# A two-layer hybrid decoder on one core: h of the SwiGLU stages turned by DMA instead of TensorE

## The chip, the cores and the metric

The kernel runs on one core of one Trainium2 chip. A core has five engines that run side by side and meet at semaphores: TensorE (PE in the profile; PEld is its weight load), VectorE (DVE), ScalarE (ACT), GpSimd (POOL) and SyncE (SP), which here issues nearly all transfers. Sixteen DMA engines move the data. The metric is the device time of one execution in microseconds (us).

## What is computed

Two layers, each `x += 1/2 SwiGLU_1(norm(x))`, then a mixer (gMLP and an indexer-selected attention side by side), then `x += 1/2 SwiGLU_2(norm(x))`, and a final norm. There are 256 tokens, 1024 channels, and 2816 hidden channels in a SwiGLU; everything is float32. Only the SwiGLUs are touched by the change:

```python
def _swiglu(h, w_gu, w_down):
    gate, up = jnp.split(h @ w_gu, 2, axis=-1)
    return (jax.nn.silu(gate) * up) @ w_down
```

So in the kernel's names h = silu(gate) * up, 256 tokens by 2816 channels, and it is the left operand of the down product.

## The kernel before

**Tiling.** Tokens are cut into two row tiles (t = 0, 1) of 128. A SwiGLU's hidden channels are cut into FC = 11 blocks (j) of 256. `proj(tiles, t, ...)` makes gate and up of one block for one row tile: the output is 128 tokens by 512 columns (256 gate, 256 up) in one PSUM bank `acc`, and the contraction over 1024 channels takes 8 steps. To keep float32 accuracy each operand is split into a coarse part (hi, xhi, hh) and the rest (lo, xlo, hl), and each product is three matmuls (`mm3`, L239): 8 x 3 = 24 matmuls for one row tile, 48 for a block. `down(j, t, ...)` multiplies h of a block by the down weights into two banks `dn` of 512 columns: 2 x 2 x 3 = 12 matmuls for one row tile.

**h.** After `proj`, `h_evac` makes h of that row tile: ScalarE the silu (`sg`, L281), VectorE the product (L283). It lies with tokens on partitions. As the left operand of `down` it must have hidden channels on partitions, so `h_trans` (L286 and following) turns its two 128x128 halves by two TensorE transposes (L289) against `ident` into a PSUM bank `tr`; then ScalarE writes the coarse part `hh` (L293) and VectorE the rest `hl` (L294).

**Order.** The software runs one block behind: after the gate/up products of block j come the first row tile's `h_trans` of block j, `down` of block j-1 for t = 0, the second row tile's `h_trans` and `down` of block j-1 for t = 1. Only the first block differs: its two `h_trans` are put into `hooks`, a list of work that `proj` runs (`run_hooks`) after three quarters of its products, here in block 1. The last two blocks' down products are made in `tail` (in the last SwiGLU, in `final`), where the second row tile of the last block is turned between them.

**Weights.** They come as 512 KB tiles into 4 buffers `raw`, loaded by SP (`issue_dma`, L111). `issue_split` makes `hi` on ScalarE (L135) and `lo` on VectorE (L136) in two halves, in 6 buffers each. `done(n)` gives tile n free, splits the next one and issues the load after that. Only the products of the second row tile call `done`, and the second half of `down` for its two tiles. Per block there are four gate/up tiles and two down tiles.

**Queues.** SP issues in the order of the program text: a load stands behind whatever was written before it. The order on TensorE, ScalarE, VectorE and GpSimd is made by a planner that follows the program text where it can; each of these engines then works through its own list in order. In the first block of layer 0 (`first`) the order is written by hand, and weights and inputs are still arriving.

Of the kernel before, what the change touches and what calls it, by code (L numbers as in the profile page):

```python
# [10 lines left out]
F32 = mybir.dt.float32  # L11
F32R = mybir.dt.float32r
I32 = mybir.dt.int32
AF = mybir.ActivationFunctionType
OP = mybir.AluOpType
AX = mybir.AxisListType
# [3 lines left out]
P = 128  # L20
# [4 lines left out]
FC = DFF // 256  # L25
# [20 lines left out]
def hybrid_kernel(ctx: ExitStack, tc: tile.TileContext, a: dict, out: bass.AP):  # L46
    nc = tc.nc
    V, S, G, PE = nc.vector, nc.scalar, nc.gpsimd, nc.tensor
# [3 lines left out]
    wspl = ctx.enter_context(tc.tile_pool(name="wspl", bufs=SPL_BUFS))  # L52
    keep = ctx.enter_context(tc.tile_pool(name="keep", bufs=1))
    work = ctx.enter_context(tc.tile_pool(name="work", bufs=2))
# [3 lines left out]
    def bank(tag, bufs):  # L58
        return psum.tile([P, 512], F32, name=tag, tag=tag, bufs=bufs)
# [60 lines left out]
    def issue_split(before=None):  # L120
        n = state["split"]
        if n >= len(specs):
            return
        while state["dma"] <= n:
            issue_dma()
        _, k, w = specs[n]
        r = raws.pop(n)
        hi = wspl.tile([P, 1024], F32R, name="hi", tag="hi")
        lo = wspl.tile([P, 1024], F32R, name="lo", tag="lo")
        m = k * w  # L130
        for b in range(2):
            c = slice(b * m // 2, (b + 1) * m // 2)
            if before is not None:
                before(b)
            S.copy(hi[:, c], r[:, c])  # L135
            V.tensor_tensor(lo[:, c], r[:, c], hi[:, c].bitcast(F32), OP.subtract)  # L136
        wts[n] = (hi[:, :m].rearrange("p (k w) -> p k w", k=k),
                  lo[:, :m].rearrange("p (k w) -> p k w", k=k))
        state["split"] = n + 1
        issue_dma()  # L140

    def take(count):
        n = state["use"]
        state["use"] = n + count
        while state["split"] < n + count:
            issue_split()
        return list(range(n, n + count))
# [23 lines left out]
    def rsqrt(dst, v, scale, eng, plus=None):  # L171
# [5 lines left out]
        else:  # L177
            eng.tensor_scalar(h, v, plus, 0.5 * scale, op0=OP.add, op1=OP.mult)
        sh = small.tile([P, 1], I32, name="rs_s", tag="rs_s")
        V.tensor_scalar(sh, h.bitcast(I32), 1, None, op0=OP.logical_shift_right)  # L180
        y = small.tile([P, 1], F32, name="rs_y", tag="rs_y")
        eng.tensor_scalar(y.bitcast(I32), sh, -1.0, RSQRT_GUESS, op0=OP.mult, op1=OP.add)
        u = small.tile([P, 1], F32, name="rs_u", tag="rs_u")
# [12 lines left out]
    def stats(t, eng=None):  # L196
        junk = work.tile([P, D], mybir.dt.bfloat16, name="junk", tag="junk", bufs=1)
        ss = small.tile([P, 1], F32, name="ss", tag="ss")
        S.activation(junk, X[t], AF.Square, accum_out=ss)  # L199
        rstd[t] = small.tile([P, 1], F32, name="rstd", tag="rstd", bufs=4)  # L200
# [16 lines left out]
    def split_gain(t, k, v, g, parts=(0, 1)):  # L217
        if 0 in parts:
            S.activation(xhi[t][:, k, :], v, AF.Copy, scale=g)  # L219
        if 1 in parts:  # L220
# [16 lines left out]
    def mm3(dst, shi, slo, whi, wlo, start, stop, between=None):  # L237
        for n, (a1, b1) in enumerate(((shi, whi), (shi, wlo), (slo, whi))):
            PE.matmul(dst, a1, b1, start=start and n == 0, stop=stop and n == 2)  # L239
            if between is not None:  # L240
                between()

    hooks, steps = [], []
# [15 lines left out]
    def proj(tiles, t, w, last, mid=True):  # L259

        ps = bank("acc", 2)
        for q, n in enumerate(tiles):
            whi, wlo = wts[n]
            for kk in range(2):
                k = 2 * q + kk
                mm3(ps[:, :w], xhi[t][:, k, :], xlo[t][:, k, :], whi[:, kk, :], wlo[:, kk, :],
                    k == 0, k == 7, step)
            if last:
                done(n)
            if q == 2 and mid:  # L270
                run_hooks()
        return ps


    def ffn_sub(l, f, gain_next, first=None, ahead=None, final=None):
        acc = [[None, None], [None, None]]
        hT = {}

        def h_evac(j, t, ps):
            sg = work.tile([P, 256], F32, name="sg", tag="sg")  # L280
            S.activation(sg, ps[:, :256], AF.Silu, scale=rstd[t])  # L281
            h = work.tile([P, 256], F32, name="h", tag="h", bufs=3)
            V.scalar_tensor_tensor(h, ps[:, 256:], rstd[t], sg, op0=OP.mult, op1=OP.mult)  # L283
            return h

        def h_trans(j, t, h):  # L286
            tr = bank("tr", 2)
            for i in range(2):
                PE.transpose(tr[:, i * P:(i + 1) * P], h[:, i * P:(i + 1) * P], ident)  # L289
            hh = wspl.tile([P, 2, P], F32R, name="hh", tag="hh", bufs=4)  # L290
            hl = wspl.tile([P, 2, P], F32R, name="hl", tag="hl", bufs=4)
            v = tr[:, :256].rearrange("p (k q) -> p k q", k=2)
            S.copy(hh, v)  # L293
            V.tensor_tensor(hl, v, hh.bitcast(F32), OP.subtract)  # L294
            hT[j, t] = (hh, hl)

        def down(j, t, tiles, last):
            hh, hl = hT[j, t]
            for n2 in range(2):
                if j == 0:  # L300
                    acc[t][n2] = bank("dn", 4)
                for kk in range(2):
                    whi, wlo = wts[tiles[kk]]
                    c = slice(n2 * 512, (n2 + 1) * 512)
                    mm3(acc[t][n2], hh[:, kk, :], hl[:, kk, :], whi[:, 0, c], wlo[:, 0, c],
                        j == 0 and kk == 0, final is not None and (j, t, n2, kk) == (FC - 3, 1, 1, 1))
            if last:
                for kk in range(2):
                    done(tiles[kk])

        for j in range(FC):
            if j == 0 and first is not None:
                p0, p1 = first()
                h0 = h_evac(j, 0, p0)
                h1 = h_evac(j, 1, p1)
            else:
                if j == FC - 3 and ahead is not None:
                    ahead()
                tiles = take(4)
                h0 = h_evac(j, 0, proj(tiles, 0, 512, False))  # L320
                h1 = h_evac(j, 1, proj(tiles, 1, 512, True))
            if j == 0:
                hooks.append(lambda h0=h0: h_trans(0, 0, h0))
                hooks.append(lambda h1=h1: h_trans(0, 1, h1))
                continue
            h_trans(j, 0, h0)
            if j < FC - 1:
                dt = take(2)
                down(j - 1, 0, dt, False)
                h_trans(j, 1, h1)  # L330
                down(j - 1, 1, dt, True)
        dt = take(4)
        js = (FC - 2, FC - 1)

        if final is not None:
            final(acc, hT, dt, lambda: h_trans(FC - 1, 1, h1))
            return

        def tail(t, n2, pre=None):
            for idx, j in enumerate(js):  # L340
                hh, hl = hT[j, t]
                for kk in range(2):
                    n = dt[2 * idx + kk]
                    whi, wlo = wts[n]
                    c = slice(n2 * 512, (n2 + 1) * 512)
                    mm3(acc[t][n2], hh[:, kk, :], hl[:, kk, :], whi[:, 0, c], wlo[:, 0, c],
                        False, idx == 1 and kk == 1)
                    if t == 1 and n2 == 1:
                        done(n)
                if pre is not None and idx == 0:  # L350
                    pre()

        tail(0, 0, pre=lambda: h_trans(FC - 1, 1, h1))
        residual(0, 0, acc[0][0], 0.5)
        tail(0, 1)
        residual(0, 1, acc[0][1], 0.5)
        new_xT(0)
        tail(1, 0, pre=lambda: xT_half(0, 0, X[0], gain_next))
        residual(1, 0, acc[1][0], 0.5)
        xT_half(0, 1, X[0], gain_next)  # L360
        stats(0)
        tail(1, 1)
        residual(1, 1, acc[1][1], 0.5)
        stats(1)
        hooks.append(lambda: next_t1(gain_next))
# [29 lines left out]
    def mixer(l, loads):  # L395
# [55 lines left out]
        def index_scores(t):  # L451
# [11 lines left out]
            for b, bk in enumerate(banks):  # L463
                r = work.tile([P, 512], F32, name="rr", tag="b2", bufs=4)
                S.activation(r, bk, AF.Relu)
                rr.append(r)
# [29 lines left out]
        def attn_scores(t):  # L496
# [14 lines left out]
            for b, bk in enumerate(banks):  # L511
# [6 lines left out]
                for i in range(per):  # L518
                    e = b * per + i
                    h = 2 * (g * per + i) + par  # L520
                    S.activation(pr[:, h, :], s[:, i, :], AF.Exp, bias=mx[:, e:e + 1],
                                 accum_out=den[:, h:h + 1])
# [89 lines left out]
        def evac(kind, c, t, ps, bias):  # L612
# [14 lines left out]
            elif c == 4:  # L627
                S.activation(vv[:, t, :], ps, AF.Copy, scale=rstd[t])
            elif c == 0:
# [277 lines left out]
```

## Time and profile before

| | us |
|---|---|
| median of 3 runs | 1122.73 |
| lowest, highest | 1122.67, 1124.02 |
| profiled execution, time | 1121.22 |
| profiled execution, span | 1119.5 |

The span runs from the first to the last recorded instruction; the time of the same execution is 1.7 us longer. The DMA engines move 206 MB, nearly all of it weights, at a mean of 184 GB/s, and TensorE's granted clock averages 0.998. What the rows below mean: a group gives line, engine, operation, the tiles written and read, the shape and the count, then the busy time in us, the mean of one in ns and the idle time in front. A row of the chain or of the timeline begins with its start and its length in us. A row of a stretch gives its length, then for each engine the busy time and the number of instructions, the granted clock, the share of time that the 16 DMA engines were busy, and GB/s. SPq is SP's queue of transfers; a row of it that joins several issues also holds the time in which it waited between them.

### The profile page before, as it was taken

The numbers are of one execution on the slowest core, as the hardware profiler recorded it, in microseconds if no ns is written. First come the engines' busy times: TensorE is split into PE (matmuls) and PEld (weight loads), VectorE is DVE, ScalarE is ACT, GpSimd is POOL, SyncE is SP. The second block draws the span as 40 slices with busy tenths as digits, with TensorE's granted clock in tenths as the row PEclk, the third lists the DMA queues.
The fourth block names the chain that finished last, engine by engine and source line by source line (L and its number), as shares of the span: only waits on it lengthen the run. The fifth ranks groups of instructions, "written<-read, shape, count | busy, mean of one in ns | idle before, by whom it ended". The sixth has DMA issues, their size and how long they took to land.

```text
span 1119.5 us, 15216 instructions
## 1 busy us (share of the span) xinstructions
PE 1108.4 (99%) x5318; PEld 924.7 (83%) x5318; DVE 735.4 (66%) x1488; ACT 607.5 (54%) x1225; POOL 36.8 (3%) x99
## 2 busy tenths in 40 slices
PE   8999999999999999999999999999999999999997
PEld 7888888888988888888888888888889888888885
DVE  7654655889958665455575555578898567465464
ACT  7554545555765654454564454464566557454453
POOL 0000000100000100000010000010000001000001
PEclk9999999999999999999999999999999999999999
DMA  8755653644655655554464555546346455555550
GB/s 298 241 189 179 221 196 136 231 151 131 184 183 175 202 188 175 202 188 173 166 222 159 206 194 199 206 157 210 132 149 203 156 182 194 182 193 188 202 188 37
DMA packets 59836, 206.28 MB, mean 184 GB/s; under 512 B 7024, under 2 KB 8432, under 8 KB 59760
## 3 DMA queue, kind: packets, MB, share of 16 engines
q1 hardware_dynamic: 59328, 204.77, 54.1%
q8 instruction: 41, 0.67, 0.2%
q10 hardware_dynamic: 432, 0.55, 0.1%
q14 instruction: 35, 0.29, 0.1%
HBM read 204.25 MB, written 1.05 MB: 183 GB/s over the span
## 4 chain that ended last, share of the span: by engine, by line
PE 97%; DVE 1%; DMA 1%; ACT 0%; issue 0%; ACTq 0%; SPq 0%
PE acc L239 62%; PE dn L239 29%; PE tr L289 2%; PE tr L210 1%; PE dn L555 1%; DMA x<-in_x_dram 1%; PE dn L504 1%; PE dn L460 1%; PE tr L545 0%; PE tr L434 0%; DMA xt<-in_xt_dram 0%; PE dn L602 0%; DVE lo L136 0%; ACT junk L199 0%; DVE rs_u L187 0%; DVE rs_y L188 0%
## 5 line engine op out<-in xcount | busy, mean ns | idle before, releaser
L136 DVE TENSOR_TENSOR lo<-raw,hi 128x512 fp32r<-128x512 f32 (+1 forms) x768 | 485.8, 678 | 134.5 <-ACT hi L135 127.5
L135 ACT CAST hi<-raw 128x512 fp32r<-128x512 f32 (+1 forms) x768 | 425.6, 613 | 168.8 <-PE acc L239 77.7
L239 PE MATMUL acc<-hi,xhi 128*128 128x512 f32 (+1 forms) x1040 | 403.5, 388 | 0.3 <-DVE h L283 0.3
L239 PE MATMUL acc<-hi,xlo 128*128 128x512 f32 (+1 forms) x1040 | 400.5, 385 | 0.0
L239 PE MATMUL acc<-lo,xhi 128*128 128x512 f32 (+1 forms) x1040 | 400.0, 385 | 0.0
L239 PEld LDWEIGHTS acc<-hi,xhi 128*128 128x128 f32 x1040 | 195.4, 188 | 37.6 <-issue 1.4
L239 PEld LDWEIGHTS acc<-hi,xlo 128*128 128x128 f32 x1040 | 195.3, 188 | 36.0 <-issue 0.7
L239 PEld LDWEIGHTS acc<-lo,xhi 128*128 128x128 f32 x1040 | 195.4, 188 | 34.9 <-issue 0.3
L239 PE MATMUL dn<-hi,hh 128*128 128x512 f32 x348 | 143.0, 411 | 0.0
L239 PE MATMUL dn<-hi,hl 128*128 128x512 f32 x348 | 136.6, 392 | 0.0
L239 PE MATMUL dn<-lo,hh 128*128 128x512 f32 x348 | 136.2, 391 | 0.0
L283 DVE SCALAR_TENSOR_TENSOR h<-acc,rstd,sg 128x256 f32<-128x256 f32 x86 | 41.6, 484 | 129.9 <-ACT sg L281 129.9
L281 ACT ACTIVATE sg<-acc,rstd 128x256 f32<-128x256 f32 x86 | 40.9, 476 | 155.0 <-PE acc L239 155.0
L239 PEld LDWEIGHTS dn<-hi,hl 128*128 128x128 f32 x348 | 65.3, 188 | 14.0
L239 PEld LDWEIGHTS dn<-lo,hh 128*128 128x128 f32 x348 | 65.7, 189 | 11.3
L239 PEld LDWEIGHTS dn<-hi,hh 128*128 128x128 f32 x348 | 65.4, 188 | 11.0
L294 DVE TENSOR_TENSOR hl<-tr,hh 128x256 fp32r<-128x256 f32 x88 | 36.7, 419 | 43.0 <-ACT hh L293 43.0
L293 ACT CAST hh<-tr 128x256 fp32r<-128x256 f32 x88 | 32.2, 370 | 59.7 <-PE tr L289 59.7
L289 PEld LDWEIGHTS tr<-ident,h 128*128 128x128 f32 x176 | 24.3, 139 | 11.0
L289 PE MATMUL tr<-ident,h 128*128 128x128 f32 x176 | 32.9, 271 | 0.0
L199 ACT ACTIVATE junk<-x 128x1024 bf16<-128x1024 f32 x13 | 13.8, 1058 | 26.4 <-DVE x L374 21.3
L219 ACT ACTIVATE xhi<-tr,gains 128x128 fp32r<-128x128 f32 x80 | 22.3, 376 | 6.5 <-PE tr L210 6.5
(141 smaller groups left out, 707.9 us busy)
## 6 DMA issues: line engine op xcount, KB each, us to landing
raw<-in_gu_dram SPq DMA_DIRECT2D x175, 512.0 KB, 4.5
raw<-in_dn_dram SPq DMA_DIRECT2D x88, 512.0 KB, 4.4
raw<-in_win_dram SPq DMA_DIRECT2D x48, 512.0 KB, 4.1
raw<-in_wg_dram SPq DMA_DIRECT2D x40, 424.0 KB, 3.8
raw<-in_wo_dram SPq DMA_DIRECT2D x16, 512.0 KB, 4.3
raw<-in_pa_dram SPq DMA_DIRECT2D x8, 512.0 KB, 5.1
raw<-in_pb_dram SPq DMA_DIRECT2D x8, 512.0 KB, 4.0
bias<-in_bg_dram SPq DMA_DIRECT2D x10, 212.0 KB, 5.4
```

What stands on the lines that cost most here:

```text
L135: S.copy(hi[:, c], r[:, c])
L136: V.tensor_tensor(lo[:, c], r[:, c], hi[:, c].bitcast(F32), OP.subtract)
L199: S.activation(junk, X[t], AF.Square, accum_out=ss)
L210: PE.transpose(tr[:, i * P:(i + 1) * P], src[:, h * 512 + i * P:h * 512 + (i + 1) * P], ident)
L219: S.activation(xhi[t][:, k, :], v, AF.Copy, scale=g)
L239: PE.matmul(dst, a1, b1, start=start and n == 0, stop=stop and n == 2)
L281: S.activation(sg, ps[:, :256], AF.Silu, scale=rstd[t])
L283: V.scalar_tensor_tensor(h, ps[:, 256:], rstd[t], sg, op0=OP.mult, op1=OP.mult)
L289: PE.transpose(tr[:, i * P:(i + 1) * P], h[:, i * P:(i + 1) * P], ident)
L293: S.copy(hh, v)
L294: V.tensor_tensor(hl, v, hh.bitcast(F32), OP.subtract)
L460: PE.matmul(banks[2 * g + par][:, i * n:(i + 1) * n], qiT[64 * par:64 * par + 64, pair, t * P:(t + 1) * P], kiT[64 * par:64 * par + 64, :n ...
```

## The change

h of all blocks but the last goes another way. `h_send` lets ScalarE copy the 16-bit halves of h's float32 words into two planes (all low halves, then all high halves), 512 16-bit elements a partition, and SP issues a transposing DMA of the 128 x 512 plane tile into `planesT`, four 128 x 128 blocks. `h_join` lets VectorE interleave the halves back into float32 `words`, now with hidden channels on partitions. `h_split`, which makes `hh` and `hl`, is the old end of `h_trans`; it now reads `words` in SBUF where it read PSUM. The new tiles use the buffers of the mixer's `sc`, `wk` and `rp2`.

The order changes too. The first row tile of a block is sent right after its `h_evac`, ahead of the second row tile's products in the program text, and the second one after its own, ahead of `down`. The first is joined after both halves of `down`, the second in the hooks of the next block's products. Block 0 sends likewise (layer 0's, whose products come from `first`, sends both tiles one after the other) and joins both in the hooks of block 1. The last block still uses `h_trans`.

```diff
+        def h_split(j, t, v):
+            hh = wspl.tile([P, 2, P], F32R, name="hh", tag="hh", bufs=4)
+            hl = wspl.tile([P, 2, P], F32R, name="hl", tag="hl", bufs=4)
+            S.copy(hh, v)
+            V.tensor_tensor(hl, v, hh.bitcast(F32), OP.subtract)
+            hT[j, t] = (hh, hl)
+
         def h_trans(j, t, h):
             tr = bank("tr", 2)
             for i in range(2):
                 PE.transpose(tr[:, i * P:(i + 1) * P], h[:, i * P:(i + 1) * P], ident)
...
+            h_split(j, t, tr[:, :256].rearrange("p (k q) -> p k q", k=2))
+
+        def h_send(h):
+
+            pl = work.tile([P, 2, 256], U16, name="planes", tag="sc")
+            S.copy(pl, h.bitcast(U16).rearrange("p (c b) -> p b c", b=2))
+            plT = work.tile([P, 4, P], U16, name="planesT", tag="wk")
+            nc.sync.dma_start_transpose(plT, pl.rearrange("p b c -> p (b c)"))
+            return plT
+
+        def h_join(j, t, plT):
+
+            w = work.tile([P, 2, P], F32, name="words", tag="rp2")
+            V.tensor_copy(w.bitcast(U16).rearrange("p k (q b) -> p b k q", b=2),
+                          plT.rearrange("p (b k) q -> p b k q", b=2))
+            h_split(j, t, w)
...
                 tiles = take(4)
                 h0 = h_evac(j, 0, proj(tiles, 0, 512, False))
+                if j < FC - 1:
+                    s0 = h_send(h0)
                 h1 = h_evac(j, 1, proj(tiles, 1, 512, True))
             if j == 0:
-                hooks.append(lambda h0=h0: h_trans(0, 0, h0))
-                hooks.append(lambda h1=h1: h_trans(0, 1, h1))
+                if first is not None:
+                    s0 = h_send(h0)
+                s1 = h_send(h1)
+                hooks.append(lambda s0=s0: h_join(0, 0, s0))
+                hooks.append(lambda s1=s1: h_join(0, 1, s1))
                 continue
-            h_trans(j, 0, h0)
             if j < FC - 1:
+                s1 = h_send(h1)
                 dt = take(2)
                 down(j - 1, 0, dt, False)
-                h_trans(j, 1, h1)
                 down(j - 1, 1, dt, True)
+                h_join(j, 0, s0)
+                hooks.append(lambda j=j, s1=s1: h_join(j, 1, s1))
+            else:
+                h_trans(j, 0, h0)
```

More of the change, by code (lines that the diff above doesn't have):

```diff
@@ L13 @@
 I32 = mybir.dt.int32
+U16 = mybir.dt.uint16
 AF = mybir.ActivationFunctionType
@@ L289, in h_trans @@
                 PE.transpose(tr[:, i * P:(i + 1) * P], h[:, i * P:(i + 1) * P], ident)
[L290 to L295, printed above, removed]
+            h_split(j, t, tr[:, :256].rearrange("p (k q) -> p k q", k=2))
[10 more added lines that the diff above has]
+            h_split(j, t, w)
         def down(j, t, tiles, last):
```

## The prediction

> **What bounds the kernel now.** I read the page's busy shares first, then the chain that ended last, then one block of a SwiGLU stage by chain, by stretch and by instruction group.
>
> ```profile
> span 1119.5 us, 15216 instructions
> PE 1108.4 (99%) x5318; PEld 924.7 (83%) x5318; DVE 735.4 (66%) x1488; ACT 607.5 (54%) x1225; POOL 36.8 (3%) x99
> PE 97%; DVE 1%; DMA 1%; ACT 0%; issue 0%; ACTq 0%; SPq 0%
> ```
>
> TensorE is busy for 99% of the span and holds 97% of the chain. A busy share can hide waits, so here is the chain through one block of layer 0's first SwiGLU:
>
> ```profile
> 147.82 0.22 PE tr L289 x2
> 148.04 2.75 PE dn L239 x12
> 150.79 0.22 PE tr L289 x2
> 151.01 2.75 PE dn L239 x12
> 153.76 10.88 PE acc L239 x48
> 164.65 0.22 PE tr L289 x2
> ```
>
> The reader is to see that nothing but TensorE work stands in it: two transposes of h, half of down, two transposes, the other half, 48 gate/up products, and the next block. The period is 164.65 - 147.82 = 16.83 us. No engine feeding TensorE is late, so TensorE work taken out shortens the kernel by its own length, as long as what replaces it stays under the remaining TensorE time. This holds for the room of the others:
>
> ```profile
> core 0: us, PE busy (x) PEld busy (x) DVE busy (x) ACT busy (x) POOL busy (x), PEclk, DMA share, GB/s
> 147.79:164.62 16.83, 16.83 (x79) 13.86 (x78) 9.29 (x18) 8.24 (x16) 0.00 (x0) 1.00 0.55 189
> L289 PE MATMUL tr<-ident,h 128*128 128x128 f32 x176 | 32.9, 271 | 0.0
> L135 ACT CAST hi<-raw 128x512 fp32r<-128x512 f32 x688 | 386.9, 621 | 156.9 <-PE acc L239 73.0 <-PE dn L239 67.8 <-issue 9.8
> L136 DVE TENSOR_TENSOR lo<-raw,hi 128x512 fp32r<-128x512 f32 x688 | 442.2, 687 | 131.7 <-ACT hi L135 124.9 <-DMA raw<-in_gu_dram 1.0
> L293 ACT CAST hh<-tr 128x256 fp32r<-128x256 f32 x88 | 32.2, 370 | 59.7 <-PE tr L289 59.7
> L294 DVE TENSOR_TENSOR hl<-tr,hh 128x256 fp32r<-128x256 f32 x88 | 36.7, 419 | 43.0 <-ACT hh L293 43.0
> ```
>
> In this block VectorE works 9.29 us, ScalarE 8.24, and the DMA engines 0.55 x 16.83 = 9.26. The granted clock is 1.00.
>
> **What goes: TensorE's transposes.** The mean of 271 ns is not the price, since matmuls overlap in the pipeline. The price is what the block takes beyond its 72 products: these run at 10.88 / 48 = 0.2267 us where nothing interrupts them, 72 of them take 16.32, and 16.83 - 16.32 = 0.51 us belongs to two pairs, 0.255 a pair. (The chain shows 0.22 of it as transposes; 0.03 is slower products after them, 2.75 us for 12 against 2.72. Were those 0.03 to stay, 0.44 a block would go, 17.6 us in all.) The 176 transposes are 88 pairs: 11 blocks by 2 row tiles by 4 SwiGLUs. The last block's 8 pairs stay. 80 go: 36 full blocks by 0.51 = 18.4 us, and the 8 pairs of the first blocks, which run inside the next block's gate products, 8 x 0.255 = 2.0. **Gain 20.4 us.**
>
> **What comes: ScalarE and VectorE.** Each of the 80 gets a ScalarE copy of 512 16-bit elements (planes) and a VectorE copy of 512 (words). No row has 16-bit strided elements. The nearest for ScalarE is the 128x512 cast, 0.62 us, and for VectorE the two-input 128x512 operation, 0.69. I take these, with bounds of a half (if elements pair up) and double (if a stride of two halves the rate). The split that follows is the old one reading SBUF in place of PSUM, so I leave it at its price. A block then costs VectorE 9.29 + 1.38 = 10.7 us and ScalarE 8.24 + 1.24 = 9.5 of 16.32; even doubled, 12.1 and 10.7. What hides them is their idle time; it costs nothing in throughput.
>
> **What comes: order and waits.** The new waits are three. SP waits for planes before it issues the transpose; VectorE waits in `h_join` for the landing; ScalarE waits for words before `hh`. What stands behind each:
>
> ```profile
> 142.92 0.48 DVE L283 SCALAR_TENSOR_TENSOR h<-acc,rstd,sg 128x256 f32<-128x256 f32 x1 [3.47 <-ACT sg L281]
> 145.75 1.69 SPq L111 DMA_DIRECT2D raw<-in_dn_dram  x2
> 148.37 0.48 DVE L283 SCALAR_TENSOR_TENSOR h<-acc,rstd,sg 128x256 f32<-128x256 f32 x1
> 148.47 8.16 SPq L111 DMA_DIRECT2D raw<-in_gu_dram  x4
> 148.48 1.15 ACT L135 CAST hi<-raw 128x512 fp32r<-128x512 f32 x2
> 153.12 2.18 ACT L135 CAST hi<-raw 128x512 fp32r<-128x512 f32 x4 [1.70 <-PE dn L239]
> 153.78 2.50 DVE L136 TENSOR_TENSOR lo<-raw,hi 128x512 fp32r<-128x512 f32 x4 [1.90 <-ACT hi L135]
> 159.75 0.48 DVE L283 SCALAR_TENSOR_TENSOR h<-acc,rstd,sg 128x256 f32<-128x256 f32 x1 [3.48 <-ACT sg L281]
> raw<-in_gu_dram SPq DMA_DIRECT2D x175, 512.0 KB, 4.5
> out_dram<-o SPq DMA_DIRECT2D x3, 256.0 KB, 2.0
> ```
>
> Row tile 0: h is ready at 142.92 + 0.48 = 143.4, planes near 144.0, and SP's next load in program order is only at 145.75, so SP isn't held. `h_join` stands after the second half of down, near 153.8, about 9 us later. Row tile 1: h at 148.85; ScalarE has the casts of 148.48 in front, to 149.63, so planes near 150.2. The transpose stands on SP between the second and third of the four gate/up loads of 148.47, whose last two wait for splits that come only after 153.12 anyway. `h_join` runs at three quarters of the next gate products, 153.76 + 18 x 0.2267 = 157.8, some 7 us after issue, in a hole of VectorE (idle from 156.28 to 159.75). By rows, a transfer lands in 2.0 us (256 KB, empty queue) to 4.5 us (a load among others); the transpose moves 128 KB, so about 3 us, or some 6 behind two loads. Both joins are met. Their products come later still: row tile 0's h of 143.4 is wanted by down after the next block's gate products, at 164.87, more than 21 us on; row tile 1's 2.75 later. If a landing were late, VectorE would hold the lo splits queued behind the join, and ScalarE the casts behind `hh`. Weights are split six tiles ahead: the first tile freed in the second row tile's products is wanted again 4.08 (the other three quarters of them) + 5.44 (down, 24 x 0.2267) = 9.5 us later, and its split takes some 2 (two casts, one lo). So a landing up to about 7 us late costs nothing. I cost the waits at 0 in the full blocks.
>
> **The DMA engines.** This decides the sign, and no transposing transfer is in the trace. In the stretch 2.60 to 3.20 us small packets ran on the ACT queue:
>
> ```profile
> q10 hardware_dynamic: 108, 0.03, 20.9%
> ```
>
> That is 0.209 x 0.6 x 16 / 108 = 18.6 ns of an engine a packet. A transpose is 128 x 512 elements of 2 bytes. If the engines move it in rows of 128 elements (256 B) it is 512 packets, 32 an engine, 0.6 us; if the writes are cut to 16 elements (32 B), 4096 packets, 256 an engine, 4.8 us at the same price. Spare engine time in a block is 16.32 - 9.26 = 7.06 us, 3.5 us for each of two transposes. I take 1.5 us, nearer the row (its packets are hundreds of bytes), and nothing for the time.
>
> By the Trainium skill ("Advanced Engine Details and Errata", X-Bar Transpose (TRN2)) such transfers run about as fast as plain ones, 350 to 400 GB/s, which would make 128 KB about 0.4 us, an estimate from that page, and leave the sum as it is; no run here shows it yet.
>
> **The start** is the one place without room. Layer 0's first block sends both tiles at once:
>
> ```profile
> 25.75 0.43 SPq L769 DMA_DIRECT2D cs<-in_rope_dram  x1
> 26.97 2.44 SPq L111 DMA_DIRECT2D raw<-in_gu_dram  x2
> 27.11 1.14 ACT L135 CAST hi<-raw 128x512 fp32r<-128x512 f32 x2
> 27.29 0.48 DVE L283 SCALAR_TENSOR_TENSOR h<-acc,rstd,sg 128x256 f32<-128x256 f32 x1
> 30.00 0.48 PE L239 MATMUL dn<-hi,hh 128*128 128x512 f32 x1
> ```
>
> The first transpose stands on SP behind the load of 25.75, so it issues near 26.2, lands at 28.2 to 30.7, and join plus split (0.69 + 0.37 + 0.42, some 1.7 with handovers) give hl at 29.9 to 32.4. Down wants it at 30.00 less the three pairs of transposes that stood ahead of it, 29.2. The second tile (h at 27.77, casts ahead until 28.25, planes 28.9) is 2 to 3 us behind, and its half of down starts 2.75 later. So a stall of 0.7 to 3.2 us, once. The gate/up loads of 26.97 stand behind the second transpose and come 2 us late, which may add one. I take 2, bounds 0 and 4; a gain is excluded, since the wait only adds. The other three SwiGLUs start with room (their second tile is wanted 13.6 us after its products end, 48 products and half a down, and by the lines above lands some 8 after).
>
> **Sum**, against the profiled execution's own 1121.2 us (span 1119.5 and 1.7 around it): 1121.2 - 20.4 + 2 = 1102.8. The median of the runs is 1.5 above that execution, so **1104.3**.
>
> **Rivals.**
>
> 1. *Full DMA engines (slower).* Where a transpose holds the engines over 3.5 us, two of them and 9.26 us of loads exceed 16.32, loads fall behind, and TensorE waits for weights in every full block. The old period is reached at (16.83 - 9.26) / 2 = 3.8 us; from there it is slower. At the upper bound, 4.8 us: 9.26 + 9.6 = 18.9, 2.0 more a block, 36 blocks, about 1195. Per-element moves would give thousands. For it: 0.55 of the engines is taken, bursts near 1.0. Against it: the nearest packets are cheap, and the bound needs eight times as many of them, smaller, at the same price. Chance 0.20. The Trainium skill speaks for it ("VectorE: DVE Perf Modes", The three transpose paths): it has a 128x128 16-bit DMA transpose at 1309 ns, four here, 5.2 us if they add up, an estimate that would make about 1230, and its rule is to prefer TensorE where PSUM will do; no row here bears on that figure.
>
> 2. *The wait moves to the joins (less gain).* Landings come over 7 us past their join, or in-order ScalarE and VectorE wait where program order isn't kept; TensorE gets its splits late by 0.1 to 0.4 us a block. 40 blocks by 0.25 = 10 lost: about 1114. For it: the loads in front of the transposes on one queue. Against: the holes above. Chance 0.13, and 0.05 that all the gain is eaten, within 0.2%, 1122.7.
>
> 3. *Hidden, as summed.* 1100 to 1109; chance 0.62.
>
> **Numbers.** A measurement of this kernel tells 0.2% (2.2 us) from no change. Faster: 0.62 + 0.13 = 0.75. Same: 0.05. Slower: 0.20. Range: 1098 (no stall at the start and a little to spare) up to 1138, which takes in rival 2, no change, and the weakest fifth of rival 1; above it stay about 0.16.
>
> **What would show it.** Right: the chain of a full block has no row of transposes, its period is 16.3, L289 has 16 transposes left, VectorE 10.7 and ScalarE 9.5 us a block, DMA share 0.65 to 0.75. Wrong: the period is over 16.4 with TensorE waiting for hi, lo or raw (rival 1, if the DMA share is near 0.95; rival 2, if VectorE's waits for the landing are long), or idle TensorE over 4 us near 30.

## The result and the profile after

| | before | after |
|---|---|---|
| median of 5 runs each | 1122.73 us | 1102.46 us |
| lowest to highest | 1122.43 to 1124.02 | 1101.43 to 1102.69 |
| profiled execution | 1121.2 us | 1101.6 us |
| ratio after / before | | 0.9817, 95% interval 0.9805 to 0.9829 |

The change takes 20.3 us off the time, 1.8%. The forecast was 1104.3. These are the page's lines of after that answer to those of before: the span, the busy shares, the shares of the chain by engine, the main DMA queue (packets, MB, share of 16 engines), and the groups that the change adds (busy us, mean ns | idle before, and what ended most of it).

```profile
span 1099.9 us, 15283 instructions
PE 1089.0 (99%) x5158; PEld 910.3 (83%) x5158; DVE 763.4 (69%) x1568; ACT 651.5 (59%) x1305; POOL 37.3 (3%) x99
...
q1 hardware_dynamic: 102848, 215.27, 60.1%
...
PE 96%; DMA 1%; DVE 1%; ACT 1%; issue 0%; ACTq 0%; SPq 0%
...
L290 ACT CAST hh<-words 128x256 fp32r<-128x256 f32 x80 | 32.4, 406 | 97.5 <-DVE words L311 97.5
...
L311 DVE COPY words<-planesT 128x512 uint16<-128x512 uint16 x80 | 36.7, 460 | 53.5 <-DMA planesT<-planes 53.5
...
L303 ACT COPY planes<-h 128x512 uint16<-128x512 uint16 x80 | 49.3, 618 | 20.7 <-DVE h L284 19.9
```

TensorE has 160 instructions fewer, the transposes, and 19.4 us less to do; the span is 19.6 shorter. It is still busy for 99%, so the gain looks like TensorE's own work and nothing else; e2_dead_pe below tests that. In the last column the new waits show: VectorE waited 53.5 us for landings and ScalarE 97.5 us for words. Whether such waits cost anything is seen only in the chain. Here it is for after, through a block of layer 0's first SwiGLU (start us, us, what), and behind it the busy time of the engines in this block and the next:

```profile
133.47 10.88 PE acc L240 x48
144.35 5.44 PE dn L240 x24
149.79 10.88 PE acc L240 x48
```

```profile
133.47:149.79 16.32, 16.32 (x73) 13.52 (x73) 9.84 (x18) 9.42 (x20) 0.64 (x1) 1.00 0.80 268
149.79:166.11 16.32, 16.32 (x73) 13.52 (x73) 9.87 (x19) 8.73 (x18) 0.00 (x0) 1.00 0.63 209
```

No row of transposes is left, no wait stands between products, and the period is 149.79 - 133.47 = 16.32 us, exactly the 72 products. VectorE works 9.9 us of it and ScalarE about 9.1; the DMA engines are busy for 0.80 and 0.63. What the waits took was idle time.

But something did move. The waits of ScalarE for gate and up weights (total us, times, longest), first before, then after, with SP's own wait ahead of the transposing transfers:

```profile
ACT hi L135 <- DMA raw<-in_gu_dram: 2.9, 4, 1.1
```

```profile
ACT hi L136 <- DMA raw<-in_gu_dram: 62.1, 47, 3.3
...
SPq L305 <- ACT hi L136: 409.3, 69, 8.1
```

And SP's own timeline through the block that begins at 133.47:

```profile
140.68 1.20 SPq L305 DMA_TRANSPOSE planesT<-planes  x1
141.97 1.00 SPq L112 DMA_DIRECT2D raw<-in_gu_dram  x2
143.06 0.99 SPq L112 DMA_DIRECT2D raw<-in_dn_dram  x2
```

Four weight loads stand right behind row tile 0's transfer. (The view above puts most of these waits down to hi; the tile that a transfer reads is planes, and here its copy ends at 140.65.) In before the same block begins at 136.94, and the first two of these loads went out 1.3 us into it:

```profile
138.27 1.53 SPq L111 DMA_DIRECT2D raw<-in_gu_dram  x2
```

Now they go out 8.5 us into it. SP stood ahead of the transfers for 409 us in all, but that is not 409 us more than before: there SP waited 846 us for buffers that `lo` sets free, here 347. What grew is ScalarE's wait for gate and up weights, from 2.9 to 62 us. TensorE does not see it: its chain through these blocks has no row of weights. The prediction had said that SP isn't held; the experiments ask what hangs on that.

### The profile page after: what moved, and what is told of

It is laid out like the page before. It is cut to its first block, busy times and chain, and to the rows that moved or that the text cites. A ratio compares the mean times of both kernels' runs of the same rounds, so it can differ in the third digit from the quotient of the medians.

```text
span 1099.9 us, 15283 instructions
## 1 busy us (share of the span) xinstructions
PE 1089.0 (99%) x5158; PEld 910.3 (83%) x5158; DVE 763.4 (69%) x1568; ACT 651.5 (59%) x1305; POOL 37.3 (3%) x99
## 3 DMA queue, kind: packets, MB, share of 16 engines
q1 hardware_dynamic: 102848, 215.27, 60.1%
## 4 chain that ended last, share of the span: by engine, by line
PE 96%; DMA 1%; DVE 1%; ACT 1%; issue 0%; ACTq 0%; SPq 0%
PE acc L240 62%; PE dn L240 29%; PE tr L211 1%; PE dn L581 1%; DMA x<-in_x_dram 1%; PE dn L530 1%; PE dn L486 1%; PE tr L571 0%; PE tr L460 0%; DMA raw<-in_gu_dram 0%; DVE lo L137 0%; DMA xt<-in_xt_dram 0%; PE dn L628 0%; ACT hi L136 0%; ACT junk L200 0%; DVE rs_y L189 0%
## 5 line engine op out<-in xcount | busy, mean ns | idle before, releaser
L136 ACT CAST hi<-raw 128x512 fp32r<-128x512 f32 (+1 forms) x768 | 430.1, 611 | 133.5 <-DMA raw<-in_gu_dram 62.1
L240 PE MATMUL dn<-hi,hh 128*128 128x512 f32 x348 | 136.8, 393 | 0.3 <-ACT hh L290 0.3
L290 ACT CAST hh<-words 128x256 fp32r<-128x256 f32 x80 | 32.4, 406 | 97.5 <-DVE words L311 97.5
L311 DVE COPY words<-planesT 128x512 uint16<-128x512 uint16 x80 | 36.7, 460 | 53.5 <-DMA planesT<-planes 53.5
L303 ACT COPY planes<-h 128x512 uint16<-128x512 uint16 x80 | 49.3, 618 | 20.7 <-DVE h L284 19.9
L291 DVE TENSOR_TENSOR hl<-words,hh 128x256 fp32r<-128x256 f32 x80 | 33.7, 422 | 17.2 <-ACT hh L290 17.0
```

Source lines behind the costliest of these rows:

```text
L303: S.copy(pl, h.bitcast(U16).rearrange("p (c b) -> p b c", b=2))
L311: V.tensor_copy(w.bitcast(U16).rearrange("p k (q b) -> p b k q", b=2), plT.rearrange("p (b k) q -> p b k q", b=2))
```

## The experiments

The edits are against the kernel after. Ratios are against runs of the kernel before on the same chip, with 95% intervals. T0 and T1 stand for the transposing transfers of row tile 0 and row tile 1. The two theories at the start: **all of the gain is TensorE's time and the replacement is hidden**, with the cliff where the prediction had put it, in the DMA engines; against it, **part of the gain is lost or made by the order of the queues**.

### What the replacement costs, and where the gain is from

**Nothing turned** (e1_no_turn): h goes straight to the split, with tokens still on partitions, so TensorE makes as many products, but the output is not the layer's.

```diff
 def h_send(h):
-    ...
+    return h
 def h_join(j, t, plT):
-    ...
+    h_split(j, t, plT.rearrange("p (k q) -> p k q", k=2))
```

> The changed kernel without any turning in the blocks that were sent by DMA: no planes, no transposing transfer, no words; h is split as it lies, so the down products use an h that was not transposed. Theory (the gain is TensorE's transposes alone, and what replaced them is hidden): the time of the changed kernel less at most the 0.6 us that the start lost, 1101.5 to 1103 us, full block 16.32 us. Rival (the replacement costs something in every block, so that more than 20 us could have been had): clearly below, 1095 us or less. Rival (a part of the gain comes from the order in which the planner now puts down, not from the transposes): can't be told here.

Measured: 1101.88 us (1101.74 to 1102.46), ratio 0.982 [0.9803, 0.9836]. That is the time of after, within its range: 80 plane copies, 80 transfers, 80 joins and all their waits are hidden to within what can be measured.

**The old TensorE pairs added back, unread** (e2_dead_pe):

```diff
-    return plT
+    return plT, h
...
 def h_join(j, t, plT):
+    plT, h = plT
+    tr = bank("tr", 2)
+    for i in range(2):
+        PE.transpose(tr[:, i * P:(i + 1) * P], h[:, i * P:(i + 1) * P], ident)
```

> The changed kernel with a pair of TensorE transposes put back at each join, whose output nobody reads; the DMA still does the turning. Theory (TensorE's own time is the whole gain): 80 pairs by 0.255 us come back, 1102.5 + 20.4 = 1122 to 1124 us, full block 16.83 us. Rival (the gain comes from the order of down or from waits on the transposes that are gone): the time stays well below, 1102 to 1112 us.

Measured: 1121.89 us (1120.76 to 1123.98), ratio 1.0002 [0.9993, 1.0012]: before's time, to a few tenths. The chain through a block:

```profile
119.74 0.22 PE tr L313 x2
...
124.08 0.22 PE tr L313 x2
...
131.13 5.44 PE dn L240 x24
136.57 0.22 PE tr L313 x2
```

The period is 136.57 - 119.74 = 16.83, as it was before. A pair costs 0.255 us wherever it stands. The new order and the new transfers are still in this kernel, so the whole gain is the pairs.

### What a transfer costs

**Each transfer twice, three times** (e4_double, e4_triple; the extra ones go to a tile that nobody reads):

```diff
 nc.sync.dma_start_transpose(plT, pl.rearrange("p b c -> p (b c)"))
+for _ in range(n - 1):
+    dead = work.tile([P, 4, P], U16, name="dead", tag="dead", bufs=2)
+    nc.sync.dma_start_transpose(dead, pl.rearrange("p b c -> p (b c)"))
```

> The changed kernel with each transposing transfer made twice, the second unread; three times gave 1131.6 us. It tells how much room the changed kernel has left behind a send. Theory (the weight loads behind a send may come about 1 us later before TensorE sees it; the twin adds 1.27 us of SP and 0.6 us of the engines): 1102 to 1108 us. Rival (no room left, the loss of the triple grows evenly from the first added transfer): 1115 us or more.

> The changed kernel with each transposing transfer made three times, the second and third into buffers that nobody reads. Theory (a transfer takes 0.69 us of all 16 engines and 1.2 us of SP, and both have room): a block needs 9.26 + 6 x 0.69 = 13.4 us of the DMA engines and 6 x 1.2 + 6 x 0.5 = 10.2 us of SP, under 16.32, so the time stays within 1102 to 1106 us, the few us more at the start, where SP holds weight loads behind the transfers. Rival (the changed kernel already sits at the edge of its loads, as the 62 us that the hi casts now wait for weights suggest): each block longer, 1115 us or more.

Measured: double 1104.79 us (1103.75 to 1104.99), ratio 0.9844 [0.9829, 0.9859]; triple 1131.55 (1128.97 to 1134.27), ratio 1.0083 [1.0063, 1.0104]. Double did as expected; triple went the rival's way, slower than before. The busy shares from 31 to 210 us, of after and of triple (the number ahead of the last is the DMA share, which is 0.75 in double):

```profile
31.00:210.00 179.00, 178.69 (x809) 148.85 (x808) 118.65 (x233) 105.73 (x214) 5.89 (x17) 1.00 0.67 218
```

```profile
31.00:210.00 179.00, 171.78 (x760) 139.41 (x759) 109.28 (x214) 101.50 (x205) 5.89 (x17) 1.00 0.85 235
```

Each further transfer adds 0.08 to 0.10 of the engines. There is room for one more beside each, at a price of 2 to 3 us that the runs barely resolve (the intervals of after and of double meet at 0.9829), and not for two. At a share of 0.85 the engines are not full, yet loads come late: ScalarE's wait for gate and up weights is 62 us in after, 90 in double, 138 in triple. Once issued, a load lands as fast in triple as in double (medians of 4.5 us for gate and up, 6.4 for down), which points at a late issue.

**Both sends late** (e6_late): T0 is sent together with T1, after row tile 1's products, so that T0 no longer stands ahead of loads in mid-block.

```diff
-                if j < FC - 1:
-                    s0 = h_send(h0)
                 h1 = h_evac(j, 1, proj(tiles, 1, 512, True))
...
             if j < FC - 1:
+                s0 = h_send(h0)
                 s1 = h_send(h1)
```

> The changed kernel with the first row tile sent after the second row tile's products instead of before them, so that in SP's order both transfers stand behind the four weight loads that those products set free. Theory (SP's order of the first transfer is what makes the weights late): same time as the changed kernel, 1101 to 1104 us, and the hi casts' waits for gate/up weights fall to less than half of 62 us. Rival (the transfer that comes later now lands after its join and VectorE holds the splits): over 1106 us.

Measured: 1102.19 us (1101.41 to 1102.48), ratio 0.9818 [0.9804, 0.9833], the same as after. The loads' wait went from the top of the waits, and the wait of words for landings rose from 53.5 to 106.8 us (the second transfer now stands behind the first: landings 2.3 / 4.7 / 6.7 us, least, median, most). Neither is on the chain.

**Three times, and late** (e4_triple_late): the two edits together, to tell full engines from a held SP.

> Each transfer three times, two of them unread, with the first row tile sent late as in the run beside this one. With the early order this was 1131.6 us. Theory (that loss was SP's order: the loads waited for planes and for 3.7 us of issue, in a ring through ScalarE's list; the DMA engines themselves have room for 9.26 + 6 x 0.69 = 13.4 us of 16.32): most of the loss goes, 1102 to 1112 us. Rival (the DMA engines, 0.85 busy in the early version, are what ran out): 1125 us or more.

Measured: 1144.02 us (1139.06 to 1149.91), ratio 1.0194 [1.0153, 1.0235]. The theory failed and the time lies on its rival's side: it became worse, not better. The DMA share is 0.85 again, landings take 4.8 us in the median and 8.7 at most. So SP held by T0 in mid-block doesn't alone explain triple. Whether it is the engines' share, SP's 1.2 us of issue for each of six transfers, or the later landings, these runs don't separate.

### What SP's order costs

**Only row tile 0 by DMA** (e3_half): row tile 1 is turned by TensorE between the halves of down, as before.

```diff
...
             if j < FC - 1:
-                s1 = h_send(h1)
                 dt = take(2)
                 down(j - 1, 0, dt, False)
+                h_trans(j, 1, h1)
                 down(j - 1, 1, dt, True)
                 h_join(j, 0, s0)
-                hooks.append(lambda j=j, s1=s1: h_join(j, 1, s1))
```

> The changed kernel with only the first row tile sent by DMA; the second is turned on TensorE between the two halves of down, as in the kernel before. Theory (each pair taken away is worth 0.255 us, independent of the other): 40 pairs by 0.255 = 10.2 us of the gain are lost, 1112 to 1113.5 us, full block 16.57 us. Rival (the second row tile's transfer, which stands between weight loads, costs time that hides part of its gain): under 1111 us. Rival (the first one's does, since SP holds weight loads behind it): over 1114.5 us.

Measured: 1145.57 us (1143.53 to 1147.33), ratio 1.0207 [1.0191, 1.0224]. Half of the change is 2% slower than none of it: the theory missed by over 30 us, and the time lies on the side of the second rival, SP's hold. Its SP timeline and its chain at one block:

```profile
102.50 1.53 SPq L112 DMA_DIRECT2D raw<-in_gu_dram  x2
112.35 1.20 SPq L305 DMA_TRANSPOSE planesT<-planes  x1
113.65 0.99 SPq L112 DMA_DIRECT2D raw<-in_gu_dram  x2
```

```profile
113.65 3.77 DMA raw<-in_gu_dram
...
117.52 0.63 ACT hi L136
...
118.17 0.69 DVE lo L137
118.87 0.41 DVE h L284
...
119.32 0.44 PE tr L297 x2
```

SP has nothing in hand from 104.03 to 112.35; it waits for the planes of row tile 0. (Its waits ahead of T0 are 308.3 us in 35 blocks, 8.8 each.) The loads behind T0 go 0.10 us after its issue ends. The cast hi of the first, its lo and then row tile 1's h stand in that order on the in-order engines; TensorE's transposes want that h at once, and down (from 119.75) stands behind them. In after the same h goes out by DMA, and down wants it only after the next block's gate and up products, so the same delay goes nowhere. (The chain puts a lo that frees a buffer ahead of the load at the same moment, so this view alone doesn't tell a held SP from a late buffer; the next run does.)

**The same half, transfers issued from ScalarE's queue** (e3_half_actq), so that nothing on SP stands behind T0:

```diff
-            nc.sync.dma_start_transpose(plT, ...)
+            nc.scalar.dma_start_transpose(plT, ...)
```

> Only the first row tile by DMA, as in the half that came out at 1145.6 us, but ScalarE's queue issues the transposing transfer, so that SP's weight loads no longer stand behind one that waits for planes. Theory (the half lost its time because SP holds the weight loads behind the transfer; hi and lo come late, VectorE's h stands behind the late lo, and the TensorE transposes of the second row tile wait for that h): the loads come in time again, TensorE waits for nothing, and each pair taken away is worth its 0.255 us: 1111 to 1114 us. Rival (the late join itself, or the transfer's DMA time, is what delays the loads, whoever issues it): it stays above 1130 us.

Measured: 1113.94 us (1112.69 to 1114.68), ratio 0.9923 [0.9908, 0.9938], as expected. ScalarE's wait for gate and up weights falls from 110.0 us in e3_half to 1.1. In the new chain a block's 48 products, half of down, one pair and the other half follow each other with no wait between. With the transfers off SP the loads go when their buffers come free, so SP's order was the cause: it makes the difference between 0.9923 and 1.0207 of before's time, some 32 us.

### What a landing costs where the engines must wait

**The full change from ScalarE's queue** (e5_actq), by the edit above alone. If holding SP were the only flaw, this would be as good as after.

> The changed kernel with all transposing transfers issued by ScalarE's queue. Theory (in the changed kernel the held loads are late but TensorE never sees it): same time, 1101 to 1103.5 us; the 62 us in which the hi casts wait for gate/up weights fall below 15. Rival (the held loads still cost the changed kernel something): below 1100 us. Rival (ScalarE has no room for 1.2 us of issue each, 9.4 + 2.4 us of 16.3 a block, or its planes copies then stand in the way): over 1106 us.

Measured: 1230.7 us (1225.69 to 1233.12), ratio 1.0949 [1.0926, 1.0973]. That is 128 us above after, and the largest miss of the study. It is also where the second rival, no room on ScalarE for the issues, had put it; e9_gate below leaves these issues in place. The chain, from the planes of T1 in one block to those in the next:

```profile
133.91 0.63 ACT planes L303
...
134.56 8.98 DMA planesT<-planes
...
143.57 0.47 DVE words L311
...
154.03 0.63 ACT planes L303
```

and ScalarE's timeline there:

```profile
134.56 1.21 ACTq L305 DMA_TRANSPOSE planesT<-planes  x1
135.81 0.41 ACT L290 CAST hh<-words 128x256 fp32r<-128x256 f32 x1 [1.28 <-DVE words L311]
144.07 0.41 ACT L290 CAST hh<-words 128x256 fp32r<-128x256 f32 x1 [7.85 <-DVE words L311]
144.38 2.17 ACT L136 CAST hi<-raw 128x512 fp32r<-128x512 f32 x4
```

In after, ScalarE's list has casts of weights at this place, and the wait at hh is short:

```profile
140.03 0.62 ACT L303 COPY planes<-h 128x512 uint16<-128x512 uint16 x1 [0.55 <-DVE h L284]
140.56 2.29 ACT L136 CAST hi<-raw 128x512 fp32r<-128x512 f32 x4
144.10 0.41 ACT L290 CAST hh<-words 128x256 fp32r<-128x256 f32 x1 [1.26 <-DVE words L311]
```

In e5_actq the period is 154.03 - 133.91 = 20.12 us, of which 8.98 is the flight of one transfer. In ScalarE's list T1's hh stands right behind T0's, which stands right behind the send. So ScalarE (and VectorE, at words) stands still for nearly the whole flight, 7.85 us, and the work behind it, the casts and splits of the next weights above all, begins when it has landed: 11.1 us to the next send. Two things met: the join right behind the send, and a flight of 9 us. The flight is long where the transfer runs beside weight loads; the DMA queues from 134.5 to 143.6 (packets, MB, share of the engines):

```profile
q1 hardware_dynamic: 414, 1.50, 66.2%
q10 hardware_dynamic: 544, 0.13, 7.9%
```

The transfer's 544 packets are 7.9% of the engines' time, 0.72 us, but in the same stretch run 414 packets of the loads. On SP's queue the loads stand behind the transfer, and it lands in 2.3 us (median). The order on SP that holds the loads also keeps them out of the transfer's way.

**Another order by shared buffers** (e8_order): e5_actq, with words and hl in one pool of three buffers, so that a join should be held until an older hl is free.

```diff
-            hl = wspl.tile([P, 2, P], F32R, name="hl", tag="hl", bufs=4)
+            hl = wspl.tile([P, 2, P], F32R, name="hl", tag="hl", bufs=3)
...
-            w = work.tile([P, 2, P], F32, name="words", tag="rp2")
+            w = wspl.tile([P, 2, P], F32R, name="words", tag="hl", bufs=3).bitcast(F32)
```

> The version with all transposing transfers on ScalarE's queue (1230.7 us), and in it words and hl share three buffers. A join can then only start when the products of down that read the buffer before have ended, so VectorE's and ScalarE's lists put the splits of the two down tiles, which the same products set free, ahead of the second row tile's join. Theory (a transfer that runs beside weight loads lands 9 us after its issue; that hurts only because the join stands ahead of those splits in in-order lists, and TensorE then waits for them): most of the loss goes, 1102 to 1115 us, though the landings stay long (median near 5, longest near 10 us). Rival (a late landing costs the time wherever the join stands): over 1190 us.

Measured: 1232.14 us (1231.37 to 1236.89), ratio 1.0979 [1.096, 1.0997]. It says nothing on the theory, because the edit did not move the join: in its timeline both hh casts still follow the send directly.

**The join bound to a later place** (e9_gate): e5_actq, and T1's join stands in the program after the next block's first products; words of row tile 1 shares its one buffer with h of the next block's row tile 0, so it can't be pulled ahead of that h's use.

```diff
...
                 if j < FC - 1:
                     s0 = h_send(h0)
+                if j:
+                    h_join(j - 1, 1, s1)
                 h1 = h_evac(j, 1, proj(tiles, 1, 512, True))
...
-                hooks.append(lambda j=j, s1=s1: h_join(j, 1, s1))
```

> The version with all transposing transfers on ScalarE's queue (1230.7 us; sharing buffers between words and hl left its lists as they were, 1232.1), now with the second row tile's join put after the next block's first products and bound to stay there: its words take the one buffer in which that block's h lay. ScalarE's list then has the four hi casts, sg, planes and a transfer between the send and the hh of the second row tile, some 5.6 us of work. Theory (the transfer's flight, 9 us beside weight loads, is dead time for VectorE and ScalarE when the join stands right behind the send; the two need 11.1 us a block besides, 20.1 in all): the flight is filled with work, the block falls back to TensorE's 16.32 us, and the time to 1101 to 1106 us, while the landings stay long (median near 5 us). Rival (a landing of 9 us costs its time wherever the join stands, or ScalarE's issue of the transfers does): over 1150 us.

Measured: 1107.69 us (1105.03 to 1110.47), ratio 0.9871 [0.9852, 0.9889], 123 us below e5_actq and a little above the expected range. ScalarE's timeline in a full block:

```profile
126.48 1.21 ACTq L306 DMA_TRANSPOSE planesT<-planes  x1
127.73 0.41 ACT L291 CAST hh<-words 128x256 fp32r<-128x256 f32 x1 [0.75 <-DVE lo L137]
...
132.87 1.21 ACTq L306 DMA_TRANSPOSE planesT<-planes  x1
134.12 0.41 ACT L291 CAST hh<-words 128x256 fp32r<-128x256 f32 x1 [1.28 <-DVE words L312]
```

The hh at 127.73 answers to a T1 issued one period earlier, at 132.87 - 16.32 = 116.55. It comes 11 us after its issue, and it did not wait for a landing. The landings are as slow as in e5_actq (2.3 / 4.9 / 10.2 us, there 2.3 / 4.9 / 10.6). The two sends above show what makes them so: T0 of 126.48 had 12 packets of loads beside it in its first 2.4 us and landed in 2.3 us; T1 of 132.87, from the same queue, had 159 and took 10.2. But work stands in the list between send and join, and in these blocks the chain is 10.88 and 5.44 again. So the loss of e5_actq was the place of the join, and not ScalarE's issues, which are the same here. What is left, by the chain, is a flight of 5.37 us at the start and four more, one in each SwiGLU at the last block that sends, whose join the edit does not bind; the first and the last of the four:

```profile
165.51 8.82 DMA planesT<-planes
...
1073.23 9.33 DMA planesT<-planes
```

### Whether more of it pays

**The heads of the mixer too** (e7_heads): q, k and the indexer's q are sent from SP and joined by VectorE, in place of four TensorE transposes and one copy.

```diff
...
-            for i in range(4):
-                PE.transpose(tr[:, i * P:(i + 1) * P], src[:, i * P:(i + 1) * P], ident)
-            S.copy(dst[:, :, t * P:(t + 1) * P], tr.rearrange("p (k q) -> p k q", k=4))
+            S.copy(pl, src.bitcast(U16).rearrange("p (c b) -> p b c", b=2))
+            nc.sync.dma_start_transpose(plT, pl.rearrange("p b c -> p (b c)"))
...
```

> The changed kernel, and in the mixers the roped q, k and indexer q (12 tiles of 128x512) are also turned by DMA from SP, planes copied when the tile is roped, joined in the hooks where TensorE turned them. Theory (the same trade: 48 transposes leave TensorE, about 0.13 us each, and the replacement hides): 6 us less, 1095 to 1098 us. Rival (in the mixer VectorE is the busiest engine beside TensorE and the roped tile comes late, so that SP holds weight loads behind the transfer): no gain or slower, 1102 us or more.

Measured: 1108.31 us (1105.99 to 1110.12), ratio 0.9876 [0.9859, 0.9893], so slower than after, against the expectation. ScalarE's wait for the mixer's input weights is 1.9 us in after, and here:

```profile
ACT hi L136 <- DMA raw<-in_win_dram: 42.9, 15, 6.5
```

The loads of these weights came late again. SP waited 46.9 us for ScalarE ahead of eight of the new transfers, with such loads behind them, which fits SP's order; that this order is the whole cause here was not tried apart.

No version beat the kernel after by more than the measurement tells; e6_late equals it.

## Why the prediction was right

The time was right because its main term was, and the main term was read from the right place. That the waits cost nothing was forecast too, but for reasons that don't hold; there it was luck. Point by point:

- **Gain 20.4 us: right.** 16.83 - 16.32 for a full block was met to the hundredth, and the fear that 0.03 a half would stay was unfounded. e2_dead_pe gives all of it back.
- **Planes and words hidden: right.** Planes cost 618 ns against 0.62 taken; words 460 ns against 0.69, mis-sized but inside its bounds. e1_no_turn shows that together with the transfers they cost nothing.
- **The DMA engines: right side, mis-sized.** Before, the same queue read

```profile
q1 hardware_dynamic: 59328, 204.77, 54.1%
```

  and with the row of after, (102848 - 59328) / 80 = 544 packets a transfer and (0.601 x 1099.9 - 0.541 x 1119.5) / 80 = 0.69 us of all 16 engines. That is next to the lower bound (0.6 us, 512 packets of 256 B), where 1.5 was taken. The page "VectorE: DVE Perf Modes" of the Trainium skill (The three transpose paths) gives 1309 ns for a 128x128 16-bit piece; four pieces adding up to 5.2 us is not what happens here: all four have landed 2.3 us after issue (median) and hold the engines for 0.69. The prediction's other estimate, 0.4 us for a transfer, lies below that. Rival 1, as priced, fell with this.
- **The start, 2 us: mis-sized.** The chains reach the first product after layer 0's first SwiGLU at these times, before and after:

```profile
193.79 3.47 PE acc L239 x18
```

```profile
189.30 3.47 PE acc L240 x18
```

  4.49 us are gained there, against 9 full blocks by 0.51 and two pairs of the first, 5.1: the start cost 0.6. The chain of after shows why:

```profile
24.71 5.11 DMA raw<-in_gu_dram
...
32.38 0.31 ACT hh L290
...
32.74 5.76 PE dn L240 x24
38.49 7.93 PE acc L240 x35
```

  Down does begin only at 32.74, when hh is there, 2.7 us later than in before; but of the 48 products that follow it 35 are left. The rest ran ahead of down, while it waited. The prediction priced the stall and overlooked that the planner fills a hole with the next block's products. Nor is it the landing that the chain names: words began at 31.10 without waiting for one, behind a `lo` that waited for the gate/up load of 24.71, and hh stood behind a planes copy in ScalarE's list.
- **"SP isn't held": wrong, and free here.** The prediction took the load that came next in time in before, the down pair at 145.75, for the next in program order. But the text has two gate/up loads between T0 and that pair; before had sent them at 138.27, ahead of T0's h. (T1 is misplaced likewise: in after it goes at 148.66, ahead of the next block's first two gate/up loads, and the next T0 stands between those and the other two.) In after SP waits ahead of 78 of the 80 transfers, and four loads stand right behind T0 in the block shown. ScalarE's wait for weights rose from 2.9 to 62 us. e3_half shows the price where something hangs on it (2% slower than before), e3_half_actq that this order was the cause.
- **"`h_join` in a hole of VectorE" and "a landing up to about 7 us late costs nothing": wrong as a rule.** VectorE does wait for the landing (53.5 us), as the planner puts joins close to their landings: in the block shown T1 issues at 148.66 and its words begin at 150.98, 2.3 us later and not 7. After is safe because the flight is 2.3 us and three or four casts stand between planes and hh, not because of a margin of 7 us behind the join. In e5_actq the join stands directly behind the send, and then the flight is dead time of two engines: the 11.1 us of work behind it and the flight must fit into 16.32, so it costs from about 5.2 us on, an estimate from e5_actq's chain (9 us there, 20.1 a block). e9_gate moves the join and takes back 123 of the 128 us with the same flights.
- **The cliff.** Rival 1 put it at full engines, 3.8 us of them a transfer, and 0.69 us is far from that. A loss came sooner, though: three transfers in place of one, 2.1 us of the engines, cost 29 us, for a reason that these runs leave open. The cliffs that they do explain are those that rival 2 names, the order on one queue and in-order engines that wait at joins; it priced them at 10 us, where e3_half lost 32 and e5_actq 128.
- **The signs.** The chain without transposes, the period and the 16 transposes left were met. VectorE takes 9.9 us a block and ScalarE 9.1, where 10.7 and 9.5 were named.

The sum for the profiled execution, 1102.8, was 1.2 above the measured 1101.6: the start's term was 1.4 too large, and 0.2 the other way is not traced.

## What to carry to other kernels

Where one engine is busy for 99% and the chain of a block holds only its instructions, as here, expect work taken out of it to pay its full time in the stream. So read the price from the block's period and not from an instruction's mean; and prove it by putting the work back unread. The transfer that came in its place was not priced by its bandwidth here: ask what stands behind its issue on that queue, and what stands between its send and its first reader on in-order engines. The same transfers gave 1102 us from one queue and 1231 from another, and half of them 1146, so look at both lists after the planner has made them, not at the trace before.

## What the runs showed of the hardware

- A transposing transfer of 128x512 16-bit elements is 544 packets (512 of 256 B would carry its 128 KB; the others were not looked into), holds the 16 engines for 0.69 us, and takes 1.2 us to issue, where a plain load takes about 0.5 (two in 1.00).
- From SP's queue it lands in 2.3 us in the median (after; 7.4 at most), from ScalarE's queue in 4.9 (e5_actq and e9_gate; 10.6 and 10.2 at most). It is not the issuer by itself: in e3_half_actq, also from ScalarE's queue but T0 alone, it is 2.4. In e9_gate, from one and the same queue, it was 2.3 with 12 packets of loads in the first 2.4 us and 10.2 with 159. "DMA: Bandwidth & Descriptors" of the Trainium skill (Issuing engines are not separate DMA queues) says that transfers of different issuers interleave on the same engines, which agrees, and that another issuer saves only issue time, which does not cover this: here the issuer also sets which loads a transfer runs beside.
- A ScalarE copy that reads every second 16-bit element takes 618 ns for 512 elements, a VectorE copy that writes every second one 460 ns.
